# A decoder trunk on one core: Q and K of one more pair of heads by Strassen products, thirteen fillers a head, exponentials and bank copies in turns, and one instruction for the last norm's scaling

## The chip, the cores and the metric

The kernel runs on one core of one Trainium2 chip. The metric is the device time of one execution in microseconds (us), lower is better. Before the change three executions took 2120.86, 2121.59 and 2122.68 us; the median is 2121.59 us.

The engines are named as the profile names them: PE multiplies matrices (PEld is its weight load, which overlaps), DVE does element-wise work on two tensors, ACT does activations and copies, POOL does the reductions across partitions and issues some DMAs, SP issues most DMAs. Each engine takes its instructions in program order and waits on semaphores for the others.

## The reference

Two layers (a gated short convolution, then dilated attention), each followed by a SwiGLU feed-forward, on a residual stream of 1024 positions and 1024 features in float32. What is touched by the change:

```python
def rms_norm(x, g):
    y = x * lax.rsqrt(jnp.mean(x * x, axis=-1, keepdims=True) + EPS)
    return y * g

BRANCHES = ((128, 1), (512, 4), (2048, 16))        # window, dilation

def dilated_attention_mixer(h, w_qkv, w_out, rel_bias):
    q, k, v = split(h @ w_qkv)                     # 16 heads x 64
    for window, dilation in BRANCHES:              # each position sees keys t - j*dilation
        s = q @ k.T * 64 ** -0.5 + rel_bias[t5_bucket(distance)]
        s = where(in_window, s, -1e30)
        lse = logsumexp(s)
        o = exp(s - lse) @ v
    alpha = softmax(lse over the three branches)
    return sum(alpha * o) @ w_out

x = x + dilated_attention_mixer(rms_norm(x, mix_norm), ...)
x = x + swiglu(rms_norm(x, ffn_norm), ...)
return rms_norm(x, final_norm)                     # the last norm
```

## The kernel before, in words

All activations lie transposed (features on partitions, positions along the row). Every matrix product with weights is made to nearly float32 precision from float32r parts: an operand is split into a high part (a copy by ACT, L144) and a low part (the difference, by DVE, L145), and three matmuls (high by high, high by low, low by high) make one product. Large projections go by Strassen's scheme: `unit_order` lists the seven products of each unit, `Strassen.mm` issues a product's matmuls (L570 to L572), DVE forms the sums of weight halves (`combo`, L192) and adds the results (L580). A plain projection goes through `product` (L372 to L374) and needs no sums.

The attention layer has three parts in time. **The Q and K phase** (`QueryKey.mix`) makes the queries and keys of the first `QK_PAIRS` = 6 pairs of heads, one Strassen unit a pair, and writes each, split and scaled by the norm, to DRAM (`emit`, L1139 to L1148). Then the values of the first pairs (`value_tiles`) are made. **The heads** follow: `slot(n, ...)` is called for n = 0 to 16. In it the PE does the scores of head n (L1573, L1574), the values product of head n-1 (L1646), and between them pieces of projections that still have to be made, the fillers: `FILL` names them in order, `fill()` yields one at a time, and a slot takes 15. A filler is a few matmuls: six of 256 columns for a piece of a value tile, three of 512 for a piece of a Q, K or output product (about one step in five of the values, and one in nine of Q and K, only empties a bank). The fillers before were two groups of values, Q and K of pairs 6 and 7 (`projections`), the last group of values, and then the first half of the output projection (`out_product`).

For a head DVE adds the bias to the scores as it takes them out of PSUM (L1584 to L1615), forms a maximum m (L1598 to L1624), POOL reduces m over the partitions (L1627), and `softmax` subtracts (DVE, L1635) and exponentiates (ACT, L1636) five pieces, in place: lf, lh, ld and two of lp. `values` multiplies the exponentials by the values, with a block of ones beside them, in two PSUM banks; ACT then takes from each bank the logarithm of the denominators (z, L1669) and the sums (o, L1670). A slot has two loops of eight steps. For n up to `LAG` = 13 the scores go with fillers in the first loop, and the values product of head n-1 in the second, where `softmax(new)` ran whole at step 3; for n over 13 the values product of head n-1 goes with the scores in the first loop, and the exponentials at step 4 of the second. All PSUM tiles come in turn from eight banks, so a bank that is read late holds up the next score that wants it.

When a pair's two heads are done, `finish` and `attended` (L1710) normalise it and write it to DRAM; `load_attended` brings pairs 0 to 3 back (tiles `oin`), and `halves` splits them (w_hi by ACT, w_lo by DVE, 1024 wide) for `out_product`. That was hung on slot `LAG - 1` = 12, steps 4 to 7 of the second loop.

**The last norm** (`final`) runs with the last down projection. For each finished piece of x, `each` squared it and multiplied it in place by the norm's weight (ACT, L1935); when 1/rms of a stretch was known, `scaled` multiplied by it (DVE, L1944) and sent the piece out.

Of the kernel before, what the change touches and what calls it, by code (L numbers as in the profile page):

```python
# [20 lines left out]
H = 16  # L21
KT = D // 128
FT = DF // 128
HALF = 512
# [17 lines left out]
FFN_PAIRS, FFN_CHUNK = 9, 3  # L42
CONV_PAIRS, CONV_CHUNK, CO = 0, 1, 4
CONV, QK = "conv", "qk"
QK_PAIRS = 6
PAGES = 41
SOFT = 4
FIN0 = 2
AO_WIDE = 5
AO = 4  # L50
LAG = 13
FILL = (("v", 0), ("v", 1), ("v", 2), ("qk", 6), ("qk", 7), ("v", 3))
DEEP_ORDER = (1, 2, 5, 6, 7, 3, 4)


# [39 lines left out]
def view(t, off, dims):  # L95
    return bass.AP(tensor=t.tensor, offset=t.offset + off, ap=[t.ap[0]] + [list(d) for d in dims])
# [3 lines left out]
def trunk(ctx: ExitStack, tc: tile.TileContext, x, gains_in, cwi, ck, cwo, wqkv, wo, relb,  # L100
# [1375 lines left out]
    def blk(j):  # L1476
        return (j // 4) * HALF + (j % 4) * 8

    def attention(norm, qk):
# [159 lines left out]
        def values(p, a, st):  # L1639
            lf, lh, ld, lp = (st[n] for n in ("lf", "lh", "ld", "lp"))  # L1640
            acc = [bank(), bank()]
            kd = [[128, 4], [1, 32]]
            b1 = [[32, 16], [1, 8]]

            def mm(ih, off, dims, u, rhs, first=False, last=False):
                nc.tensor.matmul(view(acc[ih], off, dims), vx[:, u, 64 * a:64 * a + 128], rhs,  # L1646
                                 start=first, stop=last)

            for ih in range(2):
                for r4 in range(4):  # L1650
                    mm(ih, r4 * 32, kd, 8 + r4, view(lf, ih * HALF + r4 * 32, kd), first=r4 == 0)
                    if r4 % 2:
                        yield
            for r4 in range(4):
                mm(1, r4 * 32, kd, 12 + r4, view(lh, r4 * 32, kd))
                if r4 % 2:
                    yield
            for j in range(8):
                off = (j % 4) * 8
                mm(j // 4, off, b1, j, view(ld, blk(j), b1), last=False)  # L1660
                if j:
                    mm(j // 4, off, b1, j - 1, view(lp, blk(j), b1), last=j % 4 == 3)
                yield
            o, z = st["o"], st["z"]
            n0 = slice(64 * a, 64 * a + 64)
            z0 = slice(64 - 64 * a, 128 - 64 * a)
            for ih in range(2):
                s = slice(ih * HALF, (ih + 1) * HALF)
                nc.scalar.activation(z[n0, s], acc[ih][z0], AF.Ln)  # L1669
                nc.scalar.activation(o[n0, s], acc[ih][n0], AF.Copy)  # L1670
            yield

        def finish(p):
# [42 lines left out]
        def slot(n, dense, ndense, late=0, hook=iter(())):  # L1716

            def other(k):
                for _ in range(k):
                    next(dense, None)  # L1720

            p, a = divmod(n, 2)
            if n < H:
                new = dict(bias=bias.pop(n))
                sc = scores(p, a, new)
            else:
                sc = iter(())
# [12 lines left out]
            extra = later = iter(())  # L1740
            lagged = n <= LAG
            if n + 1 < H:
                later = classes(n + 1)
            if lagged and a and p:
                ending.append(finish(p - 1))
            used = 0
            if lagged:
                for i in range(8):
                    next(sc, None)
                    if n or i % 2:  # L1750
                        other(1)
                        used += 1
                    if a and ending and i == 0:
                        run(ending.pop())
                run(sc)
            else:
                if a == 0 and not late:
                    other(1)
                    used += 1
                for i in range(8):  # L1760
                    next(sc, None)
                    next(pv, None)
                    next(pv, None)
                    if i >= late and i % 2 == 0:
                        other(1)
                        used += 1
                run(sc)
                run(pv)
                if a == 0:
                    extra = finish(p - 1)  # L1770
                if a == 0 and n < H:
                    load_values(p)
            left = max(ndense - used, 0)
            for i in range(8):
                next(pv, None)
                next(pv, None)
# [73 lines left out]
        slot(H, dense, 15)  # L1850
        run(dense)
        return acts

# [60 lines left out]
    with tc.tile_pool(name="third", bufs=1) as scope["pool"]:  # L1914
# [5 lines left out]
        def final(key, ks, hid):  # L1920
# [3 lines left out]
            def each(n, c):  # L1924

                s = slice(*c)
                if norm.acc is None:
                    norm.acc, norm.rstd = page("acc"), page("rstd")
                if n == 0:
                    nc.scalar.activation(norm.acc[:, s], X[n][:, s], AF.Square)  # L1930
                else:
                    sq = page("sq")
                    nc.scalar.activation(sq[:, s], X[n][:, s], AF.Square)
                    sums.append((sq, s))
                nc.scalar.activation(X[n][:, s], X[n][:, s], AF.Identity, scale=norm.gain(n))  # L1935

            def add_squares(keep=0):
                while len(sums) > keep:
# [2 lines left out]

            def scaled(i, n, rstd):
                s = slice(*pieces[i])
                nc.vector.tensor_tensor(out=X[n][:, s], in0=X[n][:, s], in1=rstd, op=ALU.mult)  # L1944
                (nc.sync, nc.scalar)[n % 2].dma_start(out[n][:, s], X[n][:, s])

            def some(k):
# [109 lines left out]
```

## Time and profile before

The profiled execution took 2121.1 us by its own time, and its span from first to last instruction was 2119.3 us.

| | busy us | share of the span | instructions |
|---|---|---|---|
| PE | 2088.8 | 99% | 11006 |
| DVE | 1737.2 | 82% | 3255 |
| ACT | 1023.0 | 48% | 1868 |
| POOL | 236.5 | 11% | 337 |

The stages that the change touches lie at about 930 to 1080 us (Q and K phase), 1103 to 1421 us (the heads) and 2065 to 2119 us (the last norm). A busy PE is not a PE at its peak, because matmuls overlap in the pipeline and each is shown for its whole passage: what a matmul costs is the distance from its start to the next one's. A wait shows up as idle time ahead of an instruction, with the instruction that ended it.

### The profile page before, as it was taken

The numbers are of one execution on the slowest core, as the hardware profiler recorded it, in microseconds if no ns is written. First come the engines' busy times: TensorE is split into PE (matmuls) and PEld (weight loads), VectorE is DVE, ScalarE is ACT, GpSimd is POOL, SyncE is SP. The second block draws the span as 40 slices with busy tenths as digits, with TensorE's granted clock in tenths as the row PEclk, the third lists the DMA queues.
The fourth block names the chain that finished last, engine by engine and source line by source line (L and its number), as shares of the span: only waits on it lengthen the run. The fifth ranks groups of instructions, "written<-read, shape, count | busy, mean of one in ns | idle before, by whom it ended". The sixth has DMA issues, their size and how long they took to land.

```text
span 2119.3 us, 30767 instructions
## 1 busy us (share of the span) xinstructions
PE 2088.8 (99%) x11006; PEld 1795.5 (85%) x11006; DVE 1737.2 (82%) x3255; ACT 1023.0 (48%) x1868; POOL 236.5 (11%) x337
## 2 busy tenths in 40 slices
PE   9999999999999999999999999899999999999998
PEld 7788888888888888887799999888788888888887
DVE  8898769988888888878967777786998888888876
ACT  7433427443444554446545555554544434456435
POOL 1000000110101000010322222111011001001000
PEclk9999999999999999999999999999999999999999
DMA  7322642333332576350867778855223323358432
GB/s 220 95 95 70 229 139 70 109 110 103 107 110 102 170 216 201 107 174 33 274 202 178 185 178 212 211 172 149 70 82 108 108 100 111 115 187 244 157 95 80
DMA packets 141527, 300.77 MB, mean 142 GB/s; under 512 B 48252, under 2 KB 54478, under 8 KB 141376
## 3 DMA queue, kind: packets, MB, share of 16 engines
q1 hardware_dynamic: 107488, 201.94, 32.3%
q0 software_dynamic: 26256, 82.18, 12.3%
q10 hardware_dynamic: 7632, 14.70, 1.8%
q8 instruction: 87, 1.43, 0.3%
q14 instruction: 64, 0.52, 0.1%
HBM read 208.49 MB, written 82.93 MB: 138 GB/s over the span
## 4 chain that ended last, share of the span: by engine, by line
PE 45%; DVE 5%; ACT 2%; issue 1%; POOL 1%; DMA 0%; SPq 0%; DVEq 0%; ACTq 0%; POOLq 0%
PE bank L572 8%; PE bank L570 8%; PE bank L571 8%; PE bank L1646 4%; PE bank L373 2%; PE bank L374 2%; PE bank L372 2%; PE bank L662 1%; PE bank L665 1%; PE bank L664 1%; PE bank L1516 1%; PE bank L1517 1%; PE bank L1518 1%; PE bank L1574 1%; PE bank L1573 1%
## 5 line engine op out<-in xcount | busy, mean ns | idle before, releaser
L572 PE MATMUL bank<-b,w 128*128 128x512 f32 x1952 | 760.9, 390 | 5.3 <-DVE w L145 5.0
L570 PE MATMUL bank<-b,w 128*128 128x512 f32 x1952 | 760.8, 390 | 3.5 <-ACT w L144 2.2
L571 PE MATMUL bank<-b,w 128*128 128x512 f32 x1952 | 760.4, 390 | 0.3 <-DVE b L881 0.3
L572 PEld LDWEIGHTS bank<-b,w 128*128 128x128 f32 x1952 | 366.4, 188 | 86.5 <-DVE w L145 10.4
L570 PEld LDWEIGHTS bank<-b,w 128*128 128x128 f32 x1952 | 366.6, 188 | 79.5 <-ACT w L144 3.1
L571 PEld LDWEIGHTS bank<-b,w 128*128 128x128 f32 x1952 | 366.6, 188 | 75.2 <-DVE b L881 1.4
L144 ACT ACTIVATE w<-combo 128x512 fp32r<-128x512 f32 (+2 forms) x488 | 249.7, 542 | 237.1 <-DVE combo L192 220.5
L145 DVE TENSOR_TENSOR w<-combo,w 128x512 fp32r<-128x512 f32 (+2 forms) x488 | 278.3, 584 | 37.8 <-ACT w L144 37.0
L576 ACT ACTIVATE part<-bank 128x512 f32<-128x512 f32 x186 | 110.9, 596 | 375.6 <-PE bank L572 375.2
L145 DVE TENSOR_TENSOR w<-raw,w 128x512 fp32r<-128x512 f32 (+2 forms) x342 | 189.9, 577 | 37.0 <-ACT w L144 37.0
L580 DVE TENSOR_TENSOR part<-part,bank 128x256 f32<-128x256 f32 (+1 forms) x366 | 171.9, 502 | 29.3 <-PE bank L572 16.6
L144 ACT ACTIVATE w<-raw 128x512 fp32r<-128x512 f32 (+2 forms) x342 | 167.3, 531 | 45.9 <-PE bank L572 12.2
L372 PE MATMUL bank<-w_hi,w 128*128 128x512 f32 (+1 forms) x400 | 151.1, 378 | 4.1 <-ACT w_hi L144 4.1
L373 PE MATMUL bank<-w_lo,w 128*128 128x512 f32 (+1 forms) x400 | 149.5, 374 | 1.5 <-DVE w_lo L145 1.5
L374 PE MATMUL bank<-w_hi,w 128*128 128x512 f32 (+1 forms) x400 | 149.5, 374 | 0.7 <-DVE w L145 0.7
L491 DVE TENSOR_TENSOR x<-x,bank 128x512 f32<-128x512 f32 (+1 forms) x104 | 66.5, 645 | 61.7 <-PE bank L374 60.8
L800 DVE TENSOR_TENSOR x<-x,bank 128x512 f32<-128x512 f32 x136 | 93.4, 687 | 28.2 <-PE bank L572 28.0
L192 DVE TENSOR_TENSOR combo<-raw 128x512 f32<-128x512 f32 (+1 forms) x172 | 111.8, 651 | 0.0
L372 PEld LDWEIGHTS bank<-w_hi,w 128*128 128x128 f32 x400 | 75.6, 189 | 17.0 <-ACT w_hi L144 4.5
L374 PEld LDWEIGHTS bank<-w_hi,w 128*128 128x128 f32 x400 | 75.5, 189 | 14.7 <-DVE w L145 1.6
L373 PEld LDWEIGHTS bank<-w_lo,w 128*128 128x128 f32 x400 | 75.7, 189 | 14.3 <-DVE w_lo L145 2.1
L563 DVE TENSOR_TENSOR b<-hin,b 128x512 fp32r<-128x512 f32 x126 | 79.7, 690 | 9.3 <-ACT b L562 9.2
(241 smaller groups left out, 3454.4 us busy)
## 6 DMA issues: line engine op xcount, KB each, us to landing
hin<-part SPq DMA_DIRECT2D x126, 256.0 KB
raw<-in_ffn_w_gate SPq DMA_DIRECT2D x44, 512.0 KB
raw<-in_ffn_w_up SPq DMA_DIRECT2D x44, 512.0 KB
part<-sum POOLq DMA_DIRECT2D x72, 256.0 KB, 2.3
raw<-in_ffn_w_down SPq DMA_DIRECT2D x48, 384.0 KB
raw<-in_attn_w_qkv SPq DMA_DIRECT2D x27, 512.0 KB
raw<-in_conv_w_in SPq DMA_DIRECT2D x24, 512.0 KB
part<-part POOLq DMA_DIRECT2D x36, 256.0 KB, 2.6
```

What stands on the lines that cost most here:

```text
L144: nc.scalar.activation(hi, src, AF.Copy)
L145: eng.tensor_tensor(out=lo, in0=src, in1=hi, op=ALU.subtract)
L192: eng.tensor_tensor(out=c, in0=a, in1=b, op=op)
L372: nc.tensor.matmul(b, whi[:, a], ahi[:, s], start=first, stop=False)
L373: nc.tensor.matmul(b, whi[:, a], alo[:, s], start=False, stop=False)
L374: nc.tensor.matmul(b, wlo[:, a], ahi[:, s], start=False, stop=last)
L570: nc.tensor.matmul(b, hi[:, a], bhi, start=start and k == 0, stop=False, skip_group_check=True)
L571: nc.tensor.matmul(b, hi[:, a], blo, start=False, stop=False, skip_group_check=True)
L572: nc.tensor.matmul(b, lo[:, a], bhi, start=False, stop=k == n - 1, skip_group_check=True)
L576: nc.scalar.activation(t, b, AF.Copy)
L580: nc.vector.tensor_tensor(out=t, in0=t, in1=b, op=ALU.add)
L800: nc.vector.tensor_tensor(out=X[n][:, half(h)], in0=X[n][:, half(h)], in1=b, op=ALU.add)
```

## The change

`QK_PAIRS` is 7: Q and K of pair 6 are made in the phase as a seventh Strassen unit, and its fillers are gone from `FILL`, where the last group of values now stands ahead of pair 7. A slot takes `DENSE` = 13 fillers for 15. `values` takes z and o out of the first bank as soon as that bank is done, and not after both. `softmax` is advanced by one piece a step of the second loop, from step 3 (or 4), after the step's part of the values product. The oin splits are hung on slot `LAG - 2` = 11, steps 0 to 3. In the last norm `scaled` multiplies by weight and 1/rms in one DVE instruction, and the ACT multiplication is gone.

```diff
-QK_PAIRS = 6
+QK_PAIRS = 7
-FILL = (("v", 0), ("v", 1), ("v", 2), ("qk", 6), ("qk", 7), ("v", 3))
+FILL = (("v", 0), ("v", 1), ("v", 2), ("v", 3), ("qk", 7))
+DENSE = 13
@@ values
+            o, z = st["o"], st["z"]
+            n0 = slice(64 * a, 64 * a + 64)
+            z0 = slice(64 - 64 * a, 128 - 64 * a)
             for j in range(8):
                 off = (j % 4) * 8
                 mm(j // 4, off, b1, j, view(ld, blk(j), b1), last=False)
                 if j:
                     mm(j // 4, off, b1, j - 1, view(lp, blk(j), b1), last=j % 4 == 3)
+                if j % 4 == 3:
+                    s = half(j // 4)
+                    nc.scalar.activation(z[n0, s], acc[j // 4][z0], AF.Ln)
+                    nc.scalar.activation(o[n0, s], acc[j // 4][n0], AF.Copy)
                 yield
-            for ih in range(2):
-                s = slice(ih * HALF, (ih + 1) * HALF)
-                nc.scalar.activation(z[n0, s], acc[ih][z0], AF.Ln)
-                nc.scalar.activation(o[n0, s], acc[ih][n0], AF.Copy)
             yield
@@ slot, second loop
-                if i == (3 if lagged else SOFT):
-                    if n < H:
-                        live[n] = new
-                        run(softmax(new))
-                if i >= SOFT:
+                if i < 4:
                     next(hook, None)
+                if i == (3 if lagged else SOFT) and n < H:
+                    live[n] = new
+                    soft = softmax(new)
+                next(soft, None)
                 other(left * (i + 1) // 8 - left * i // 8)
             run(pv)
+            run(soft)
             run(extra)
@@ the calls of slot
-            if n == LAG - 1:
+            if n == LAG - 2:
                 done.update(load_attended(range(AO)))
-            hook = halves() if n == LAG - 1 else iter(())
-            slot(n, dense, 15, 3 if n == H - 2 else 0, hook)
+            hook = halves() if n == LAG - 2 else iter(())
+            slot(n, dense, DENSE, 3 if n == H - 2 else 0, hook)
@@ final
-                nc.scalar.activation(X[n][:, s], X[n][:, s], AF.Identity, scale=norm.gain(n))
-                nc.vector.tensor_tensor(out=X[n][:, s], in0=X[n][:, s], in1=rstd, op=ALU.mult)
+                nc.vector.scalar_tensor_tensor(X[n][:, s], rstd, norm.gain(n), X[n][:, s], op0=ALU.mult, op1=ALU.mult)
```

What it does to the order on ACT, in the second loop of a slot: the exponentials of head 2 and the copies of head 1's two banks, before:

```order
L1636 ACTIVATE lf<-lf 128x1024
L1636 ACTIVATE lh<-lh 128x512
L1636 ACTIVATE ld<-ld 128x1024
L1636 ACTIVATE lp<-lp 128x16x24
L1636 ACTIVATE lp<-lp 128x512
L1669 ACTIVATE z<-bank 64x512
L1670 ACTIVATE o<-bank 64x512
L1669 ACTIVATE z<-bank 64x512
L1670 ACTIVATE o<-bank 64x512
```

The same nine instructions in the changed kernel (its line numbers are one higher here):

```order
L1637 ACTIVATE lf<-lf 128x1024
L1669 ACTIVATE z<-bank 64x512
L1670 ACTIVATE o<-bank 64x512
L1637 ACTIVATE lh<-lh 128x512
L1637 ACTIVATE ld<-ld 128x1024
L1669 ACTIVATE z<-bank 64x512
L1670 ACTIVATE o<-bank 64x512
L1637 ACTIVATE lp<-lp 128x16x24
L1637 ACTIVATE lp<-lp 128x512
```

The first bank's copies moved ahead of four exponentials, the second bank's ahead of two.

On DVE, the end of slot 12 before: the last two instructions that form m, the five subtractions (mb is POOL's maximum), the four low parts of oin, and the first additions for head 13:

```order
L1623 TENSOR_TENSOR m<-m,ld 128x512
L1624 TENSOR_TENSOR m<-m,lp 128x512
L1635 TENSOR_TENSOR lf<-lf,mb 128x1024
L1635 TENSOR_TENSOR lh<-lh,mb 128x512
L1635 TENSOR_TENSOR ld<-ld,mb 128x1024
L1635 TENSOR_TENSOR lp<-lp,mb 128x16x24
L1635 TENSOR_TENSOR lp<-lp,mb 128x512
L145 TENSOR_TENSOR w_lo<-oin,w_hi 128x1024 x4
L1584 TENSOR_TENSOR lf<-bank,bias 128x4x64 x4
```

And the end of slot 11 in the changed kernel, where they now stand:

```order
L1624 TENSOR_TENSOR m<-m,ld 128x512
L1625 TENSOR_TENSOR m<-m,lp 128x512
L146 TENSOR_TENSOR w_lo<-oin,w_hi 128x1024 x4
L1636 TENSOR_TENSOR lf<-lf,mb 128x1024
L1636 TENSOR_TENSOR lh<-lh,mb 128x512
L1711 TENSOR_TENSOR o<-o,z 128x1024
L1636 TENSOR_TENSOR ld<-ld,mb 128x1024
L1636 TENSOR_TENSOR lp<-lp,mb 128x16x24
L1636 TENSOR_TENSOR lp<-lp,mb 128x512
L1142 SCALAR_TENSOR_TENSOR kq<-bank,rstd 128x512
```

The four low parts moved one slot earlier, and from behind the subtractions into the place between m and the first subtraction.

More of the change, by code (lines that the diff above doesn't have):

```diff
@@ L1662, in values @@
                     mm(j // 4, off, b1, j - 1, view(lp, blk(j), b1), last=j % 4 == 3)
+                if j % 4 == 3:
+                    s = half(j // 4)
+                    nc.scalar.activation(z[n0, s], acc[j // 4][z0], AF.Ln)
+                    nc.scalar.activation(o[n0, s], acc[j // 4][n0], AF.Copy)
                 yield
-            o, z = st["o"], st["z"]
-            n0 = slice(64 * a, 64 * a + 64)
-            z0 = slice(64 - 64 * a, 128 - 64 * a)
-            for ih in range(2):
-                s = slice(ih * HALF, (ih + 1) * HALF)
-                nc.scalar.activation(z[n0, s], acc[ih][z0], AF.Ln)
-                nc.scalar.activation(o[n0, s], acc[ih][n0], AF.Copy)
             yield
@@ L1739, in slot @@
                 pv = iter(())
-            extra = later = iter(())
+            extra = later = soft = iter(())
             lagged = n <= LAG
@@ L1849, in attention @@
         ensure(ahead_ao)
-        slot(H, dense, 15)
+        slot(H, dense, DENSE)
         run(dense)
```

## The prediction

> **What bounds the kernel now.** I read the page's first part, then the matmuls of an undisturbed stretch, then what PE waited for among the heads, then the order on ACT and DVE around those waits, and last the final norm.
>
> The page says that PE is never idle for long. To see whether it is full, I take the list by lines for a stretch of 150 us without idle time (760 to 910 us) and look at the count.
>
> ```profile
> PE 2088.8 (99%) x11006; PEld 1795.5 (85%) x11006; DVE 1737.2 (82%) x3255; ACT 1023.0 (48%) x1868; POOL 236.5 (11%) x337
> L570 PE MATMUL bank<-b,w 128*128 128x512 f32 x221 | 86.0, 389 | 0.0
> ```
>
> L570, L571 and L572 follow each other in the loop, so 663 matmuls went by in 150 us: one of 512 columns costs 0.226 us, not the 389 ns of its row, which overlaps its neighbours. The kernel is a queue of matmuls, and an edit gains by taking matmuls out or by taking waits away. The waits of PE's weight loads in the heads' 318 us (the waits view; the weight load stands first at a wait, so its idle time is the whole gap):
>
> ```profile
> PEld bank L372 <- ACT w_hi L144: 4.5, 2, 3.9
> PEld bank L1573 <- ACT o L1670: 3.3, 3, 1.3
> PEld bank L373 <- DVE w_lo L145: 2.1, 2, 1.1
> PEld bank L1573 <- ACT v L1521: 0.9, 3, 0.5
> ```
>
> That is 10.8 us. Two of these rows (4.5 and 2.1) are the first matmuls of `out_product`, which wait for the oin splits. The windows view just behind that wait (columns: window, length, busy time of PE, PEld, DVE, ACT and POOL, granted clock, DMA):
>
> ```profile
> 1341.00:1345.00 4.00, 0.28 (x3) 0.09 (x1) 2.06 (x4) 3.84 (x7) 0.00 (x0) 1.00 0.15 38
> 1345.00:1347.00 2.00, 1.23 (x3) 0.82 (x4) 1.92 (x2) 2.00 (x3) 1.39 (x3) 0.76 0.16 35
> 1347.00:1350.00 3.00, 3.00 (x14) 2.72 (x13) 1.66 (x2) 2.14 (x5) 0.79 (x2) 0.59 0.60 152
> ```
>
> After four idle microseconds the granted clock was 0.76 and then 0.59: 2 x 0.24 + 3 x 0.41 = 1.7 us more. So the heads lose 12.5 us. The Trainium skill (TensorE: Matmul & The Clock Gate, Part 1: The HAM clock gate) says the same, half clock after an idle window of about 3.4 us; these rows agree.
>
> The second row of waits is the banks. The timeline of ACT, and of PE, where head 3's scores begin (start, length, then the instruction and its idle time):
>
> ```profile
> 1153.73 1.07 ACT L1636 ACTIVATE lf<-lf 128x1024 f32<-128x1024 f32 x1 [7.82 <-DVE lf L1635]
> 1154.70 0.61 ACT L1636 ACTIVATE lh<-lh 128x512 f32<-128x512 f32 x1
> 1155.53 1.06 ACT L1636 ACTIVATE ld<-ld 128x1024 f32<-128x1024 f32 x1 [0.22 <-DVE ld L1635]
> 1156.49 1.03 ACT L1636 ACTIVATE lp<-lp 128x384 f32<-128x384 f32 x2
> 1157.54 0.59 ACT L1669 ACTIVATE z<-bank 64x512 f32<-64x512 f32 x1
> 1158.14 0.59 ACT L1670 ACTIVATE o<-bank 64x512 f32<-64x512 f32 x1
> 1159.37 0.59 ACT L1670 ACTIVATE o<-bank 64x512 f32<-64x512 f32 x1
> 1158.78 0.39 PE L1573 MATMUL bank<-qa,ka 128*128 128x256 f32 x1 [1.10 <-ACT o L1670]
> ```
>
> PE resumes as the first o copy ends. That copy stood behind all five exponentials, which stood behind DVE's subtractions. So the second engine to watch is DVE. Its timeline around that place, then POOL's part in its waits (waits view, slots 0 to 11), then those slots whole, and slot 1 alone:
>
> ```profile
> 1152.47 1.23 DVE L1635 TENSOR_TENSOR lf<-lf,mb 128x1024 f32<-128x1024 f32 x1 [3.50 <-POOL mb L1627]
> 1156.42 1.41 DVE L1584 TENSOR_TENSOR lf<-bank,bias 128x256 f32<-128x256 f32 x4
> 1167.93 1.23 DVE L1635 TENSOR_TENSOR lf<-lf,mb 128x1024 f32<-128x1024 f32 x1 [3.44 <-POOL mb L1627]
> DVE lf L1635 <- POOL mb L1627: 35.3, 11, 3.5
> DVE w_lo L145 <- ACT w_hi L144: 9.3, 4, 3.5
> DVE kq_lo L1147 <- ACT kq_hi L1144: 3.6, 4, 1.3
> 1103.10:1325.80 222.70, 219.53 (x1694) 209.91 (x1693) 168.43 (x305) 118.16 (x168) 62.16 (x56) 1.00 0.77 191
> 1115.40:1134.00 18.60, 18.60 (x161) 18.43 (x160) 14.68 (x27) 8.84 (x14) 5.79 (x6) 1.00 0.95 234
> ```
>
> From the first addition to the next subtraction is 11.5 us, of which 3.4 is waiting for POOL, and the subtractions take 4.0: a head costs DVE 15.5 us in a row, with nothing else in it. A slot costs PE 18.6 us with fifteen fillers. DVE was busy 168.4 us in twelve slots and waited 35.3 + 9.3 + 3.6 in the chain: 216.6 of 222.7 us. It looks three quarters busy and is nearly full.
>
> **The change part by part.**
>
> *The seventh pair in the phase.* A Strassen unit has 7 products x 4 tiles x 3 = 84 matmuls of 512 columns; the fillers that go were 2 projections x 2 halves x 8 x 3 = 96. Twelve fewer at 0.226 are **-2.7 us**, if the phase hides its new DVE work. The windows of the phase's middle and end:
>
> ```profile
> 990.00:1050.00 60.00, 59.24 (x259) 48.04 (x258) 59.83 (x95) 32.77 (x57) 15.51 (x28) 1.00 0.62 206
> 1050.00:1080.00 30.00, 30.00 (x134) 24.86 (x133) 25.49 (x40) 16.19 (x27) 7.56 (x14) 1.00 0.61 211
> ```
>
> DVE is full in the middle, where early sums pile up, but has come down to 85% at the end, where one unit follows another, with PE never idle. The new unit comes there, so I price it at nothing beyond its 19 us of matmuls. If the pile were still there, PE would lose some of what the middle loses, 0.8 us in 60; I allow 0 to 3.
>
> *Thirteen fillers and the order of exponentials and copies.* No matmul goes with this; it decides which waits remain. Head 2's chain of exponentials began at 1153.73 and the first bank was free at 1158.73, 5.0 us later. With the copies behind lf alone that is 1.07 + 0.6 + 0.6 = 2.3 us. The second bank was free after 6.2 us; behind three exponentials it is 1.0 + 1.2 + 0.6 + 1.1 + 1.2 = 5.1. So PE may run some 1 to 2.7 us further ahead before a bank stops it. Against it: with two fillers fewer PE takes less time a slot. The step of a value filler is six matmuls at 0.12, in four steps of five:
>
> ```profile
> 1152.82 0.28 PE L1516 MATMUL bank<-w_hi,b 128*128 128x256 f32 x1
> 1152.94 0.28 PE L1517 MATMUL bank<-w_lo,b 128*128 128x256 f32 x1
> ```
>
> That is 0.58 on the mean, so 18.6 becomes 17.4 us, and 1.9 us are left beside DVE's 15.5 for weight splits, o times z and the rest.
>
> I count twelve slots. PE: pair 6's 36 steps are gone (32 x 3 x 0.226 = 21.7 us) and twelve value steps move in (7.0), so 219.5 becomes 204.8. DVE loses pair 6's two 1024-wide splits and its four `emit`s, whose prices stand in this timeline of slot 6 (and, for two such splits undisturbed, in the last row, of slot 8):
>
> ```profile
> 1222.19 1.04 DVE L1139 TENSOR_TENSOR kq<-bank,rstd 128x512 f32<-128x512 f32 x1
> 1223.06 3.47 DVE L145 TENSOR_TENSOR w_lo<-raw,w_hi 128x1024 fp32r<-128x1024 f32 x2
> 1226.46 0.68 DVE L1147 TENSOR_TENSOR kq_lo<-kq,kq_hi 128x512 fp32r<-128x512 f32 x1
> 1222.44 3.22 POOL L1627 PARTITION_ALL_REDUCE mb<-m  x1 [6.36 <-DVE m L1624]
> 1273.16 2.36 DVE L145 TENSOR_TENSOR w_lo<-raw,w_hi 128x1024 fp32r<-128x1024 f32 x2 [3.54 <-ACT w_hi L144]
> ```
>
> 2.4 for the splits, 4 x 1.6 for the emits, some 4 of their waits for ACT: -12.8. It gains the four oin splits, 4.7 us, which fill the 3.4 us of a POOL wait in slot 11. The same rows show what that costs: two splits beside POOL's reduction took 3.47 us, without it 2.36. So the four take 1.1 more, and add 4.7 + 1.1 - 3.4 = 2.4. DVE's chain becomes 216.6 - 12.8 + 2.4 = 206 us against PE's 205. The two are level, so some of the 12.5 us will stay. (The Trainium skill, GPSIMD Engine Reference, Key points, has POOL and VectorE contend for SBUF when a DVE instruction has two SBUF inputs; a split has, and these rows agree. Without that rule the chain would be 1.1 shorter.)
>
> What goes: both oin rows and the half clock, 4.5 + 2.1 + 1.7 = 8.3, since the splits now finish a slot before the first output product asks. What stays: of the bank rows' 4.2 I keep 2, because heads 1 and 2 have DVE as late as now. And at the slots 12 and 13, behind the oin splits, DVE falls behind by the 2.4 of slot 11 and by about 1 a slot of emits (slots 9 to 11); PE can run ahead of it some way (it was in head 3's slot at 1152.82 and DVE's first addition came at 1156.42, with the bank copies the only wait), so I charge 2.5. Left over: 4.5, or **-8.0 us**. The bounds: nothing is left, -12.5; or DVE's chain holds every slot, all of 4.2 stays and about 6 come from slots 9 to 13, which leaves -2.
>
> *The last norm.* Three ACT multiplications stand in the chain that ends the kernel, each ahead of a sum or of 1/rms for which DVE waits:
>
> ```profile
> 2100.10 0.51 ACT L1935 ACTIVATE x<-x,gains 128x256 f32<-128x256 f32 x1
> 2100.52 0.40 ACT L144 ACTIVATE sum<-acc 128x256 fp32r<-128x256 f32 x1
> 2104.12 0.51 ACT L1935 ACTIVATE x<-x,gains 128x256 f32<-128x256 f32 x1
> 2105.48 0.42 DVE L1944 TENSOR_TENSOR x<-x,rstd 128x256 f32<-128x256 f32 x1 [1.56 <-ACT rstd L487]
> L1252 DVE SCALAR_TENSOR_TENSOR hcol<-x,gains,rstd 128x512 f32<-128x512 f32 x16 | 11.9, 750 | 3.4 <-ACT rstd L487 3.4
> L1944 DVE TENSOR_TENSOR x<-x,rstd 128x512 f32<-128x512 f32 x8 | 5.5, 690 | 2.1 <-ACT rstd L487 2.1
> ```
>
> Each holds the next ACT instruction up by 0.42 (2100.10 to 2100.52); with one more ahead of the first 1/rms that is -1.3 at most. DVE pays: the fused form takes 750 where the product takes 690 ns, 0.06 on eight pieces and half of that on sixteen, at most +1.0, all on DVE's own chain at the end. Net between -1.3 and +1.0; I take **-0.4**, since the last eight read 1/rms from PSUM and the fused form of L1252 reads SBUF, so part of the 1.0 may not come.
>
> *The sum.* 2119.3 - 2.7 - 8.0 - 0.4 = 2108.2 us of span. Around the span lie 1.8 us (2121.1 by its own time), so 2110.0; the profiled run lies 0.5 under the median of the three, 2121.59, so I forecast **2110.5 us**.
>
> **The rivals.** *All waits go* (chance 0.08): PE gets far enough ahead everywhere, -12.5, and 2106. For it: the bank rows count three waits each in sixteen heads. Against it: the two level chains.
>
> *DVE becomes the bound of the heads* (0.20): the waits for w_hi do not fall with pair 6, or the pieces of softmax, now mixed with splits, add their ACT waits to DVE's chain. Then slots 1 to 13 run at DVE's pace, 8 to 13 us of waiting stay, and the time is 2115 to 2120; a bit under half of that is within 0.2%.
>
> *Slower, by late exponentials in the last three heads* (0.12). In slots 14 to 16 the values product asks at once for exponentials that a lagged slot may deliver a whole loop later. They are now spread over the second loop, and PE reaches them with two fillers less. If DVE comes into slot 14 more than 5 us late (the subtraction of lf lies 6 to 7 us ahead of DVE's next addition, and its exponential is ready 2.3 after it), PE waits there, and again in slots 15 and 16, up to 4 us each with the half clock's 1.7 behind it, 17 us at the worst. Against -2.7 and the 8.3 of the oin wait that makes +6, or 2128; it is slower than before from 11 us of such waits on, and by more than 0.2% from 15. Against it: these slots have four to eight fillers between.
>
> *The change does nothing in the phase*, since PE's matmuls do fall by twelve, is excluded by count.
>
> **How the numbers follow.** Forecast, 0.60: 2107 to 2115 (its own bounds -2 to -12.5 for the waits, without the ends). The range takes in the most of the second rival: 2105.5 to 2119. A measurement here tells 0.2%, or 4.2 us, from no change: faster is below 2117.3. Faster has the forecast, all waits gone, and 0.09 of the DVE rival: 0.77. Same is the other 0.11 of it. Slower, the late exponentials: 0.12.
>
> **What would show it.** PE should have 10994 matmuls and the same 0.226; no wait of L372 for the oin splits, and no stretch of half clock among the heads; slots 1 to 11 at 17.0 to 18 us; the waits for o smaller but not gone, and DVE's first additions 4 to 6 us behind PE in slots 2, 6 and 12; the w_lo of oin beside the reduction at more than 1.2 us. The phase's seventh unit should add 19.0 us. I am wrong if L1646 waits in slots 14 to 16, if the phase shows new waits for weights, or if a slot takes 19 us with PE idle in it.

## The result, and the profile after

| | before | after |
|---|---|---|
| median of 17 runs, us | 2121.6 (2120.8 to 2123.7) | 2118.2 (2115.2 to 2121.4) |
| profiled execution, own time / span, us | 2121.1 / 2119.3 | 2115.9 / 2114.2 |
| head 0 starts / feed-forward starts, us | 1103.1 / 1473.5 | 1122.1 / 1469.7 |

The ratio of after to before is 0.9984, with a 95% interval of 0.9977 to 0.9991. The change gains 3.4 us; 11.1 were forecast, and 2118.2 lies inside the range (2105.5 to 2119.0) near its upper end, and above the forecast's own 2107 to 2115.

The first part of the page shows that the twelve matmuls are gone (11006 before):

```profile
PE 2084.8 (99%) x10994; PEld 1791.6 (85%) x10994; DVE 1745.5 (83%) x3267; ACT 1012.1 (48%) x1852; POOL 236.7 (11%) x337
```

What PE's weight loads waited for among the heads after the change (waits view, 1122 to 1421 us: total, times, longest):

```profile
PEld bank L1574 <- ACT o L1670: 7.0, 6, 1.6
PEld bank L1574 <- ACT v L1522: 3.7, 4, 1.5
PEld bank L1647 <- ACT lf L1637: 0.3, 1, 0.3
```

Both rows of the oin splits (4.5 and 2.1) are gone, but the banks, 4.2 us before, now stop PE for 10.7. DVE's waits in slots 0 to 11, and those slots whole (windows view: busy time of PE, PEld, DVE, ACT, POOL):

```profile
DVE lf L1636 <- POOL mb L1628: 34.6, 11, 3.5
DVE w_lo L146 <- ACT w_hi L145: 10.2, 3, 4.5
...
1122.10:1334.10 212.00, 205.05 (x1653) 198.34 (x1652) 160.85 (x294) 116.34 (x164) 59.64 (x50) 1.00 0.78 187
```

The waits for w_hi are three in place of four, and not shorter in sum. The longest one, on ACT and on DVE, at the end of slot 1 (timeline; slot 2 begins on PE at 1151.0):

```profile
1156.78 0.62 ACT L1637 ACTIVATE lp<-lp 128x512 f32<-128x512 f32 x1
1157.30 1.05 ACT L145 ACTIVATE w_hi<-raw 128x1024 fp32r<-128x1024 f32 x1
...
1152.74 1.15 DVE L1636 TENSOR_TENSOR lp<-lp,mb 128x384 f32<-128x384 f32 x2
1158.38 1.22 DVE L146 TENSOR_TENSOR w_lo<-raw,w_hi 128x1024 fp32r<-128x1024 f32 x1 [4.48 <-ACT w_hi L145]
1159.52 1.41 DVE L1585 TENSOR_TENSOR lf<-bank,bias 128x256 f32<-128x256 f32 x4
```

DVE had finished head 1's subtractions at 1153.9 and stood 4.5 us for the high part of a value slab. Behind that stood the first addition of head 2, which came 8.5 us after PE's first score. One slot later PE has no free bank (timeline, the three waits of slot 3):

```profile
1175.53 0.19 PEld L1574 LDWEIGHTS bank<-qa,ka 128*128 128x128 f32 x1 [1.47 <-ACT o L1670]
1178.36 0.19 PEld L1574 LDWEIGHTS bank<-qa,ka 128*128 128x128 f32 x1 [1.59 <-ACT o L1670]
1179.93 0.19 PEld L1574 LDWEIGHTS bank<-qa,ka 128*128 128x128 f32 x1 [1.04 <-ACT v L1522]
```

So the row that says "ACT o" names the end of a chain that began with DVE's wait for w_hi, about one slot earlier (PE stops at 1174.1, 15.7 us after that wait ends). The other two waits for w_hi end at 1213.1 and 1266.2 us, and PE's next bank waits of over 1 us end at 1232.5 and 1287.8. That the first cause the second is tested in runs 1 and 5.

### The profile page after: what moved, and what is told of

It reads as the page before. It is cut to its first block, busy times and chain, and to the rows that moved or that the text cites. A ratio compares the mean times of both kernels' runs of the same rounds, so it can differ in the third digit from the quotient of the medians.

```text
span 2114.2 us, 30745 instructions
## 1 busy us (share of the span) xinstructions
PE 2084.8 (99%) x10994; PEld 1791.6 (85%) x10994; DVE 1745.5 (83%) x3267; ACT 1012.1 (48%) x1852; POOL 236.7 (11%) x337
## 3 DMA queue, kind: packets, MB, share of 16 engines
q0 software_dynamic: 26256, 82.18, 12.3%
## 5 line engine op out<-in xcount | busy, mean ns | idle before, releaser
L573 PE MATMUL bank<-b,w 128*128 128x512 f32 x1980 | 771.7, 390 | 5.3 <-DVE w L146 5.0
L571 PE MATMUL bank<-b,w 128*128 128x512 f32 x1980 | 771.7, 390 | 3.3 <-ACT w L145 2.3
L572 PE MATMUL bank<-b,w 128*128 128x512 f32 x1980 | 771.3, 390 | 0.3 <-DVE b L882 0.3
L573 PEld LDWEIGHTS bank<-b,w 128*128 128x128 f32 x1980 | 371.7, 188 | 87.6 <-DVE w L146 10.4
L571 PEld LDWEIGHTS bank<-b,w 128*128 128x128 f32 x1980 | 371.9, 188 | 80.2 <-ACT w L145 3.1
L572 PEld LDWEIGHTS bank<-b,w 128*128 128x128 f32 x1980 | 371.9, 188 | 76.5 <-DVE b L882 1.2
```

The source lines that it names most:

```text
L571: nc.tensor.matmul(b, hi[:, a], bhi, start=start and k == 0, stop=False, skip_group_check=True)
L572: nc.tensor.matmul(b, hi[:, a], blo, start=False, stop=False, skip_group_check=True)
L573: nc.tensor.matmul(b, lo[:, a], bhi, start=False, stop=k == n - 1, skip_group_check=True)
```

## The experiments

Line numbers of kernels that hold deferred low parts are 13 to 16 higher. Each run shares its chip with runs of the kernel before, and its ratio is to them.

### 1. Low parts of weights made in POOL's wait

```diff
 add_slab
-        ops.append((key, lambda: split(get_raw(i)[:, :src.shape[1]])))
+        later = key[:2] in (("v", 1), ("v", 2), ("v", 3), ("qkv", NPAIR - 1))
+        ops.append((key, lambda: (split_later if later else split)(get_raw(i)[:, :src.shape[1]])))
 slot, between the two loops; value_tiles and projections, behind take
+            lows()
```

`split_later` issues the copy on ACT and keeps the subtraction in a list; `lows` issues what is in it.

> The changed kernel, with one edit: ACT still makes the high part of a value slab's or of pair 7's weights where it did, but DVE makes the low part only in front of the next head's first subtraction, where it waits 3.5 us for POOL's maximum. No instruction more or less. Theory A (the new order on ACT puts w_hi behind copies and exponentials, DVE stands still for it in its serial chain, comes late with the next head's additions and then PE is stopped by the banks): DVE's 12.1 us of waiting for w_hi fall under 2, its first addition in slot 2 comes at most 6 us behind PE (8.5 in the changed kernel), PE's weight loads wait for o and v at most 5 us among the heads (10.7), and the time falls by 5 to 8 us, to 2110 to 2113 beside the 2118.2. The low parts beside the reduction should take 3.4 us a pair and the reduction 4.0. Theory B (thirteen fillers give PE too little to do beside any chain of DVE): the waits for o and v stay at 9 us or more and the time falls by less than 2 us.

Measured: 2109.0 us (2108.8 to 2111.1), ratio to before 0.9941 (0.9929 to 0.9954); span 2107.0. DVE's and PE's waits in slots 0 to 11, those slots whole, and a pair of low parts beside the reduction:

```profile
DVE lf L1651 <- POOL mb L1643: 25.9, 11, 4.2
...
PEld bank L1589 <- ACT v L1537: 1.6, 3, 0.7
PEld bank L1589 <- ACT o L1685: 0.4, 1, 0.4
...
1122.10:1326.90 204.80, 203.68 (x1652) 198.19 (x1651) 167.74 (x295) 115.72 (x164) 62.07 (x50) 1.00 0.80 194
...
1162.08 4.05 DVE L190 TENSOR_TENSOR w_lo<-raw,w_hi 128x1024 fp32r<-128x1024 f32 x2
```

No wait for w_hi is left in these slots. They take 204.8 us, as the prediction's count of PE's work had it, and DVE's first addition in slot 2 is 2.9 us behind PE. A pair of low parts beside the reduction takes 4.05 us and not the 3.4 expected. The gain of 9.2 by the medians is larger than theory A's 5 to 8; between the two profiles it is 7.2 (spans of 2114.2 and 2107.0), and run 9 bears on the other 2. Theory B would have kept the waits and falls.

### 2. The old order with thirteen fillers, 3. the new order alone

```diff
 2: after, softmax in slot                    3: before, softmax in slot
-                    soft = softmax(new)      -                        run(softmax(new))
-                next(soft, None)             +                        soft = softmax(new)
+                    run(softmax(new))        +                next(soft, None)
 and z, o of both banks behind the loop       and z, o at j == 3 and j == 7
```

> The changed kernel with the old order on ACT and DVE: the five exponentials in one piece at step 3, and z and o of both banks behind the whole values product. Seven pairs in the phase, thirteen fillers, the oin splits in slot 11 and the new last norm stay. Theory A: the split of weights in slot 1 waits about 1.9 us for w_hi again in place of 4.5, DVE's waits for w_hi fall from 12.1 to 5 to 9, the bank waits of PE (o and v, 10.7) fall to 4 to 8, and the time is 2 to 6 us under the changed kernel's 2118.2, so 2112 to 2116. Theory B (the fillers): without the earlier copies the banks come free 1 to 3 us later in each slot, the bank waits rise over 12 us, and the time is 2119 to 2124.

> The kernel before with the new order alone (z and o bank by bank, one piece of softmax a step); six pairs, fifteen fillers, oin splits in slot 12, old last norm. Theory A: DVE's waits for w_hi rise from 9.3 us to 14 or more, since its high parts stand behind copies here too; fifteen fillers cover most of it, so PE's bank waits (4.2) stay within 3 to 8 and the time is 2120 to 2125, no better than before. Theory B (the order is good by itself, and the fillers are what costs): bank waits 4.2 to 2, time 2118.5 to 2120.

Measured: run 2 took 2120.5 us (ratio 0.9998, 0.9989 to 1.0006). Run 3 took 2131.7 (1.0049, 1.0035 to 1.0062), slower than before. In run 2 DVE's waits for w_hi in slots 0 to 11, and ACT at the same place in slot 1:

```profile
DVE w_lo L146 <- ACT w_hi L145: 10.9, 3, 4.8
...
1153.43 1.02 ACT L1637 ACTIVATE lp<-lp 128x384 f32<-128x384 f32 x2
...
1154.85 0.59 ACT L1670 ACTIVATE z<-bank 64x512 f32<-64x512 f32 x1
...
1156.68 0.59 ACT L1671 ACTIVATE o<-bank 64x512 f32<-64x512 f32 x1
1157.18 1.05 ACT L145 ACTIVATE w_hi<-raw 128x1024 fp32r<-128x1024 f32 x1
```

So half of theory A falls: with the old order the wait is as long (4.8 us), because w_hi stands behind the four copies here too. In the kernel before, the same split stood ahead of them (its ACT and DVE, end of slot 1):

```profile
1134.94 1.03 ACT L1636 ACTIVATE lp<-lp 128x384 f32<-128x384 f32 x2
1135.88 1.04 ACT L144 ACTIVATE w_hi<-raw 128x1024 fp32r<-128x1024 f32 x1
1136.94 0.60 ACT L1669 ACTIVATE z<-bank 64x512 f32<-64x512 f32 x1
...
1136.95 1.23 DVE L145 TENSOR_TENSOR w_lo<-raw,w_hi 128x1024 fp32r<-128x1024 f32 x1 [1.94 <-ACT w_hi L144]
```

The splits are issued by filler count, and the groups of values come first in `FILL` both before and after: with fifteen fillers a slot this split came between the exponentials and the copies, with thirteen behind both. (No run has the change with fifteen fillers and nothing else altered, so this is read from the order and not tested by itself.) Given thirteen, the new order is worth 2.3 us (2120.5 to 2118.2).

Run 3 lies 9.3 us over the kernel before by the two profiles: 4.2 in slot 12, 2.7 in slot 13 and 2.4 in slots 0 to 11. Slot 12 loses on the oin splits, which run 3 leaves there and which there alternate with the pieces of softmax. PE's waits in slots 12 and 13, and DVE's low parts:

```profile
PEld bank L372 <- ACT w_hi L144: 6.4, 4, 3.8
PEld bank L373 <- DVE w_lo L145: 4.1, 4, 1.1
...
1346.97 1.22 DVE L145 TENSOR_TENSOR w_lo<-oin,w_hi 128x1024 fp32r<-128x1024 f32 x1 [3.32 <-ACT w_hi L144]
1348.11 1.22 DVE L1635 TENSOR_TENSOR ld<-ld,mb 128x1024 f32<-128x1024 f32 x1
1351.40 1.23 DVE L145 TENSOR_TENSOR w_lo<-oin,w_hi 128x1024 fp32r<-128x1024 f32 x1 [2.07 <-ACT w_hi L144]
```

DVE subtracts, ACT exponentiates and copies, DVE waits for that copy, and so four times over: 10.5 us of waits beside 6.6 before. Run 2's time is where theory B put it, and B's reason is borne out: PE's waits for o and v come to 13.1 us (B said over 12), and counted from PE's start of slot 2 the two banks of head 0 are free 2.6 and 1.1 us later than in the changed kernel. Run 3's time lies beyond what either theory expected.

### 4. The last norm alone

```diff
-                nc.scalar.activation(X[n][:, s], X[n][:, s], AF.Identity, scale=norm.gain(n))
-                nc.vector.tensor_tensor(out=X[n][:, s], in0=X[n][:, s], in1=rstd, op=ALU.mult)
+                nc.vector.scalar_tensor_tensor(X[n][:, s], rstd, norm.gain(n), X[n][:, s], op0=ALU.mult, op1=ALU.mult)
```

> The kernel before with the new last norm alone: one DVE instruction multiplies by weight and 1/rms, the ACT multiplication is gone. The prediction had -0.4 us. If the two traces are read rightly (the last matmul 0.7 us earlier than the rest of the change explains, and a tail after it shorter by 0.7), it is -1.4: a span of 2117.9 beside 2119.3, the stretch from the last matmul to the end 11.3 beside 12.0 us, and a median of about 2120.2. Nothing ahead of 2065 us moves by more than 0.3.

Measured: 2121.0 beside 2122.1, ratio 0.9994 (0.9985 to 1.0003), which does not exclude no change. The traces are finer. From the feed-forward's first matmul to the end it took 644.7 us here and 644.5 in the changed kernel, 645.9 before. The end of the chain, before and then after (DVE's timeline):

```profile
2111.08 0.17 DVE L1963 RECIPROCAL r<-r 128x2 f32<-128x2 f32 x1 [1.44 <-ACT r L1962]
...
2111.62 1.42 DVE L1944 TENSOR_TENSOR x<-x,rstd 128x256 f32<-128x256 f32 x4
2113.02 2.74 DVE L1944 TENSOR_TENSOR x<-x,bank 128x256 f32<-128x256 f32 x8
```

```profile
2105.75 0.17 DVE L1964 RECIPROCAL r<-r 128x2 f32<-128x2 f32 x1 [1.44 <-ACT r L1963]
...
2106.29 1.66 DVE L1945 SCALAR_TENSOR_TENSOR x<-rstd,gains,x 128x256 f32<-128x256 f32 x4
2107.88 3.22 DVE L1945 SCALAR_TENSOR_TENSOR x<-bank,gains,x 128x256 f32<-128x256 f32 x8
```

Counted from the feed-forward's start (1473.5 and 1469.7), the last 1/rms is 1.5 us earlier; the twelve pieces behind it take 0.7 longer, and the writing out behind them takes 0.4 less, which is not explained. Together that is -1.3; in this run alone -1.1.

### 5. Low parts in the next slot's first loop

```diff
 slot, first loop, in place of the call between the loops
                     next(sc, None)
+                    if i == 2:
+                        lows()
```

> As the run e1_gap, but DVE makes the low parts of the value slabs and of pair 7's weights in the next slot's first loop, behind the first additions (lf, lh), and not in POOL's wait: w_hi has long been written there, so its wait is gone, but the six low parts' 1.2 us each stay in DVE's chain. Theory C (thirteen fillers a slot put a split of weights behind the softmax of the same slot, where DVE stands 2 to 4.8 us for w_hi with the next head's additions behind it; the order of copies has no part in that): the waits for w_hi fall from 12.1 to 2.5 us or less, the waits for POOL stay near 41, PE's waits for o and v fall from 10.7 to 3 to 7, and the time is 2110 to 2114. Rival D (e1_gap gained because work was put into POOL's wait, the wait for w_hi being no matter): time 2115 to 2118.

Measured: 2111.6 us (2110.8 to 2113.9), ratio 0.9951 (0.9939 to 0.9964). Slots 0 to 11:

```profile
DVE lf L1651 <- POOL mb L1643: 35.1, 11, 3.7
...
DVE w_lo L190 <- ACT w_hi L189: 2.6, 3, 1.8
...
PEld bank L1533 <- DVE w_lo L190: 2.8, 2, 1.5
```

POOL's waits stay whole and the time is still 6.6 us under the changed kernel's: theory C holds, rival D falls. The 2.8 us in which PE waits for a low part itself are the price of this place, and about the distance to run 1 (2.6).

### 6. The oin splits alone, 7. six pairs with all the rest, 10. the same with values first

```diff
 6, on the kernel before
-            if n == LAG - 1:
+            if n == LAG - 2:
                 done.update(load_attended(range(AO)))
-            hook = halves() if n == LAG - 1 else iter(())
+            hook = halves() if n == LAG - 2 else iter(())
 and next(hook, None) at steps 0 to 3, ahead of softmax
 7: 6, with the edits of 1 and 4
 10: 7, and
-FILL = (("v", 0), ("v", 1), ("v", 2), ("qk", 6), ("qk", 7), ("v", 3))
+FILL = (("v", 0), ("v", 1), ("v", 2), ("qk", 6), ("v", 3), ("qk", 7))
```

> The kernel before with the oin splits alone moved: one slot earlier, in steps 0 to 3 of the second loop, ahead of the exponentials. The term of the prediction: both oin rows (4.5 and 2.1) and the half clock (1.7) go, which is 8.3 us less, 2113.8 beside 2122.1, if nothing comes back. If DVE's 6.3 us for four low parts beside the reduction (3.5 of them in POOL's wait) make slots 12 and 13 late, 1 to 2.5 us of bank waits come back: 2114.5 to 2116.5. If DVE's chain is the bound there in any case, 4 us or more come back: 2118 or more.

> The kernel before (six pairs, fifteen fillers, old order) with three edits: oin splits one slot earlier, the new last norm, and the low parts of the value slabs and of pairs 6 and 7 in POOL's wait as in e1_gap. It lacks what is left of the change: the seventh pair in the phase, thirteen fillers, the new order. If those are worth the twelve matmuls they save and nothing else, it lies 2.7 us over e1_gap (2109.0): about 2111.7. If thirteen fillers cost cover that fifteen give, it is at 2109 or under. If pair 6's fillers keep DVE's chain too long, it is 2114 or more, with bank waits of over 5 us in slots 3 to 10.

> e7_six_pairs_gap with the fillers in another order: the last group of values ahead of pair 7 (as the changed kernel has it), so that it is in DRAM before head 12's values are loaded. In e6_oin_alone and e7_six_pairs_gap PE stood 2.3 to 2.7 us for that load in slot 13, with the clock at half behind it. If that is what came back there, the wait goes and the time falls by 2.3 + 1.7 = 4.0 us to 2107.8; the seventh pair and thirteen fillers of the changed kernel would then be worth nothing beside e1_gap's 2109.0, since what the twelve matmuls save goes into waits. If pair 7's keys now come late for slot 14, PE waits there and the time stays at 2111 or more.

Measured: run 6, 2118.0 us (ratio 0.9981, 0.9972 to 0.9990), so 3.9 of the 8.3 came. What came back is neither of the two things expected, but a load in slot 13 (PE's timeline, SP's waits, and the window behind it):

```profile
1355.94 1.29 PE L1646 MATMUL bank<-lf,vx 128*128 128x128 f32 x5 [2.31 <-DMA vx<-vdram]
...
SPq L1533 <- DMA vdram<-v: 15.6, 1, 15.6
...
1356.00:1358.00 2.00, 2.00 (x10) 2.00 (x11) 0.00 (x0) 0.00 (x0) 2.00 (x1) 0.52 1.13 242
```

With the old `FILL` the last values are in DRAM so late that SP waits 15.6 us to load them, and PE 2.3 for the load, with the clock at 0.52 behind it. Slot 12 is 6.5 us shorter than in the kernel before, and slot 13 is 2.6 longer. In the kernel before, SP waited 12.4 us for the same values, but PE came to slot 13 later by the wait for oin and did not have to wait for the load. The changed kernel, with its values first, has no such wait.

Run 7 took 2111.8 us (0.9951, 0.9939 to 0.9964), as expected if only the twelve matmuls separate it from run 1; but it holds the same wait for the load (2.3 us), which run 1 has not, and fewer bank waits (2.2 us beside 4.4), so the agreement is partly chance. Run 10 was to remove it and fall to 2107.8. It took 2115.1 (0.9971, 0.9959 to 0.9982): the load's wait went, and pair 7's emits now met the oin splits in slot 11. PE's one large wait in slot 12:

```profile
1334.43 0.29 PEld L1588 LDWEIGHTS bank<-qa,ka 128*128 128x128 f32 x1 [5.25 <-ACT o L1685]
```

DVE's first addition in that slot came 8.9 us late, and the clock fell to 0.50 behind the wait.

### 8. Run 1 with the old order, 11. run 10 with the new one

> e1_gap with the old order of exponentials and copies (all five exponentials at step 3, z and o behind the whole values product). The changed kernel lost 2.3 us by that (2120.5 beside 2118.2). If the earlier copies help only where DVE is late, it lies within 1 us of e1_gap, 2108 to 2110; if they help in every slot, 2 to 4 us over it, with PE's waits for o in more than five places.

> e10_six_pairs_values_first with the new order of exponentials and bank copies. With thirteen fillers that order gained 2.3 to 2.9 us; alone in the kernel before it lost 9.6, of which 7 in slots 12 and 13, where the oin splits then stood among the pieces of softmax. Those are now a slot earlier and ahead of the pieces, so the loss there should be gone: 0 to 1.5 us under e10_six_pairs_values_first if earlier banks help with fifteen fillers too, the same if PE never waits for a bank any more, and 1 us or more over it if the pieces of softmax, each behind an ACT copy, still make DVE later.

Measured: run 8 took 2111.9 us (0.9950, 0.9937 to 0.9964), 2.9 over run 1, and run 11 2112.4 (0.9960, 0.9947 to 0.9974), 2.7 under run 10. In run 8 PE waits for o in six places among the heads, 3.1 us, and for v in three, 3.1; run 1 had 2.2 and 1.6. Run 11 gains more than the 0 to 1.5 us expected. So the earlier copies gain 2.3 to 2.9 us by the medians in three pairs of kernels, once the oin splits stand ahead of the pieces of softmax. In each pair the two intervals overlap a little; it is the agreement of the three that speaks for the gain.

### 9. The changed kernel again

> The changed kernel once more, unaltered. Its executions spread from 2115.2 to 2121.4 us, more than those of any other kernel here (e1_gap 2108.8 to 2111.1), and the one profiled lay 2.3 under their median. If the spread comes from waits in the heads that in some executions last long enough for the clock to fall, a second profile nearer the median (2117.5 to 2119) shows bank waits in the same slots (3, 6, 9) and a stretch of half clock of some 3.4 us behind one of them, 1.7 us each; if it comes from elsewhere, the heads take the same 299 us and the difference stands ahead of 1122 or behind 1420 us.

Measured: 2119.9 us, span 2118.1. Its waits in slot 3 are those of the first profile to a hundredth (1.47, 1.59 and 1.04 us). The windows around them, first profile above, this one below (the third number from the end is the granted clock):

```profile
1174.00:1176.00 2.00, 0.74 (x7) 0.53 (x6) 2.00 (x4) 1.94 (x4) 0.00 (x0) 1.00 1.27 231
1176.00:1178.00 2.00, 0.97 (x9) 0.77 (x7) 1.97 (x6) 1.95 (x4) 0.00 (x0) 1.00 1.04 229
1178.00:1180.00 2.00, 0.82 (x5) 0.60 (x5) 2.00 (x6) 1.95 (x5) 0.00 (x0) 1.00 0.90 175
1180.00:1182.00 2.00, 2.00 (x17) 2.00 (x18) 1.97 (x5) 2.00 (x3) 1.82 (x4) 1.00 0.50 110
```

```profile
1175.00:1177.00 2.00, 0.74 (x6) 0.64 (x6) 2.00 (x4) 1.94 (x5) 0.00 (x0) 1.00 1.29 244
1177.00:1179.00 2.00, 0.82 (x7) 0.61 (x6) 1.97 (x6) 1.95 (x3) 0.00 (x0) 1.00 1.03 227
1179.00:1181.00 2.00, 0.96 (x5) 0.76 (x6) 2.00 (x6) 1.95 (x5) 0.00 (x0) 0.81 0.82 160
1181.00:1183.00 2.00, 2.00 (x10) 2.00 (x11) 1.97 (x6) 2.00 (x4) 1.99 (x4) 0.50 0.54 127
```

Ten matmuls in 2 us in place of seventeen: slot 3 takes 24.1 us here and 21.2 there. Of the 3.9 us between the two spans 2.9 are that; 0.8 stand ahead of head 0. The stretch of low clock is some 7 us long, twice what was expected. This is one execution.

### 12. The product of o and 1/z on POOL

```diff
-                nc.vector.tensor_tensor(out=o, in0=o, in1=z, op=ALU.mult)
+                nc.gpsimd.tensor_tensor(out=o, in0=o, in1=z, op=ALU.mult)
```

> e1_gap with one instruction of each pair moved from DVE to POOL: the product of o and 1/z (1024 wide), behind POOL's maximum and ahead of its own DMA. DVE's chain loses 1.2 us in every second slot. PE's remaining waits in e1_gap are in slots 12 to 14 (2.5 us in all); if DVE's chain is what makes them, half of that goes: 2107.5 to 2108.5. If POOL's product is slow and runs beside DVE's splits or makes the next maximum late, DVE waits longer for POOL and the time is 2109.5 to 2112.

Measured: 2134.5 us (1.0058, 1.0045 to 1.0070), 25.5 over run 1. POOL's timeline in slot 6:

```profile
1229.68 2.40 POOL L1726 TENSOR_TENSOR o<-o,z 128x1024 f32<-128x1024 f32 x1 [7.63 <-DMA ka<-kq]
...
1244.15 3.24 POOL L1643 PARTITION_ALL_REDUCE mb<-m  x1 [6.57 <-issue]
```

DVE's waits for POOL among all heads:

```profile
DVE lf L1651 <- POOL mb L1643: 53.4, 14, 9.8
```

The product takes 2.4 us, as against 1.22 on DVE, and the maximum behind it comes 6.6 us later in its slot than in run 1, with DVE waiting 9.8 us for it. The whole trace shows the same: POOL stands idle 7.2 to 9.9 us ahead of each of the seven products, and 6.1 to 8.8 us ahead of the reduction that follows each. The nine reductions that follow no product start 0.1 to 0.3 us after DVE's last part of m; of the seven that follow one, five start 3.1 to 6.5 us after it. DVE's waits for POOL are 53.4 us in place of run 1's 32.5, and these 20.9 us more come near the 25.5 lost. So the maximum does come late, as the second case expected, but by far more than was expected. Why POOL stands idle whenever it goes from the one instruction to the other was not settled.

## Why the prediction was right or wrong

**Twelve matmuls, -2.7: right.** The count fell by twelve and head 0 starts 19.0 us later, as reckoned; the seventh unit's DVE work is hidden.

**The oin splits, -8.3: they went, as predicted.** No such wait and no half clock behind it stands in either profile of the changed kernel. The four low parts beside the reduction took 6.3 us (5.8 reckoned) and the reduction itself 4.0 in place of 3.2:

```profile
1327.61 6.32 DVE L146 TENSOR_TENSOR w_lo<-oin,w_hi 128x1024 fp32r<-128x1024 f32 x4
...
1327.89 4.02 POOL L1628 PARTITION_ALL_REDUCE mb<-m  x1 [1.22 <-DVE m L1625]
```

The charge of 2.5 for slots 12 and 13 is met in size, 1.8 + 0.3 + 0.3 of PE's waits behind 1334 us, but by luck: they lie in slots 13 and 14 and none in slot 12, and that the oin splits make them was not shown. What the prediction had not seen is that the move depends on the order of `FILL`: without the values ahead of pair 7, which the change also moves, 3.9 of the 8.3 came (run 6).

**The order of the copies: right.** At the end of slot 1 the two banks are free 2.3 and 5.0 us after the first exponential starts (2.3 and 5.1 reckoned). Run 2 puts 2.3 us on it.

**"Of the bank rows' 4.2 I keep 2": the step that failed.** In slots 0 to 11 PE waited 9.5 us for banks. The reason given was that DVE's chain would come down to 206 us and PE's work to 205, so that little could be late. Both sums were right: 160.9 busy + 34.6 + 10.2 + 1.2 of waits make 206.9, and PE was busy 205.05. The twelve slots took 212.0 all the same. Slots 1 to 11, forecast at 17.0 to 18 us, took 16.9 to 21.2. A sum over twelve slots lets an early slot pay for a late one, and that does not happen here: DVE cannot start on scores that PE has not made, and PE cannot go on past eight banks. The sum also hid where the waits lie. Of the "some 4 of their waits" that were to go with pair 6, those of the emits went (2.4 us, from 3.6 to 1.2); those for w_hi rose, from 9.3 in four places to 10.2 in three, since the splits that remain came to stand behind a slot's exponentials and copies. With those waits away slots 0 to 11 take 204.8 us (run 1) and 206.7 (run 5), about what PE's work takes. By the medians these runs are 9.2 and 6.6 us under the changed kernel, and the forecast was missed by 7.7.

**The rival that came true** is that DVE becomes the bound of the heads, with its first reason (the waits for w_hi do not fall). Its second, the pieces of softmax among the splits, is what run 3 shows in slot 12, but not what the changed kernel suffers from: its w_hi waits are the same in the old order. The rival of late exponentials in slots 14 to 16 did not come: 0.3 us of waiting for lf in all. Two figures of the rival that came true are off in the prediction itself: 8 to 13 us of waiting give 2114 to 2119 by its own terms and not 2115 to 2120, and the part of it within 0.2% is a bit over half (0.11 of 0.20), not under.

**The last norm, -0.4: mis-sized.** It is -1.3 by the traces. The -1.3 for ACT came whole and a little more (1.5). DVE's price is 0.7 on the last twelve pieces, within the 1.0 allowed; but a fused piece of 256 columns costs 0.06 us more than the product alone, with an operand in PSUM too, and not half of that. The writing out took 0.4 less.

**The clock.** The prediction gave the half clock to the one long wait for oin. The waits in slot 3 brought it back in the profile nearer the median, 2.9 us, and not in the first. Without it the change gains 5.2 (2121.1 to 2115.9); the median gains 3.4. That this is the cause in the other executions, whose mean clocks lie between those two, was not shown by a profile of each.

In sum: -2.7, -8.3 and -1.3 came, which would be -12.3; the banks took back 6.5 (4.2 to 10.7), and what remains, some 0.7, is put down to new waits of 0.3 us each. That leaves the 5.1 between the two profiled spans (2119.3 and 2114.2).

## What to carry to other kernels

When two chains are level in their sums, the waits are set by the slot in which one is latest and by the number of buffers between them: look there, and not at the sum. (The number of buffers was not varied here.) A wait of PE for the reader of a buffer is to be followed back through that reader; here it ended at a two-operand instruction that stood in an in-order queue right behind the copy it needs, and issuing it later, into an existing wait, gained more than the whole change (2109.0 us, the best version found). Changing how many fillers go into a slot moves every instruction that is issued by filler count, so each of them is to be looked up at its new place on every engine.

## What the hardware showed that was not expected

Behind three waits of 1.47, 1.59 and 1.04 us within 6 us, with PE busy 2.5 of the 6, the granted clock was at half (0.50) for some 7 us in one execution (run 9) and at 1.00 in another, with these three waits equal. In run 6 it was at 0.52 behind a single wait of 2.3 us. The Trainium skill (TensorE: Matmul & The Clock Gate, Part 1: The HAM clock gate) has half clock follow an idle window of about 3.4 us, and calls the window free-running. A free-running window would fit that the same waits count once and not another time. The length does not fit: none of these waits is that long, and here the measurement decides.

A partition reduction on POOL beside DVE's two-operand subtractions takes 4.0 us in place of 3.2, and the subtractions take longer too: two low parts beside it took 4.05 us together (run 1), apart from it 2.36 (the kernel before, slot 8). So both sides pay.
